# The compression's first layer in half-blocks with contiguous operands, in a hybrid decoder step on one core

## The chip, the cores and the metric

The kernel runs on one core of a Trainium2 chip. The metric is the device time in microseconds (us) of one execution. Each version is timed in several runs, and the median counts. The engines are TensorE (PE in the rows, its weight loads PEld), VectorE (DVE), ScalarE (ACT), GpSimd (POOL) and SyncE (SP, which issues the transfers). Each takes its instructions in the order written, and waits where one of them has to wait.

## The reference

One layer of a decoder for two groups of requests: a prompt of 1024 tokens and 8 samples of 8 new tokens, each sample with 512 tokens behind it in a paged cache. One projection feeds a gated convolution, a gated DeltaNet and a sparse attention with three branches (compressed, selected, window); then an output projection, a layer norm, a convolutional feed-forward block and another layer norm. All of it is in float32. The change concerns the compression of keys and values, for the prompt's tokens and for each sample's cached ones:

```python
def compress_blocks(rows, pe, w1, b1, w2):
    b, t_pad, kvh, hd = rows.shape
    r = rows.reshape(b, t_pad // CMP_STRIDE, CMP_STRIDE, kvh, hd)      # CMP_STRIDE = 16
    blocks = jnp.concatenate([r[:, :-1], r[:, 1:]], axis=2) + pe[:, None, :]
    hid = jax.nn.gelu(jnp.einsum('bclhd,lde->bche', blocks, w1) + b1)   # l = 0..31, d = e = 64
    return jnp.einsum('bche,ed->bchd', hid, w2)
```

A block is 32 tokens long and a new one starts every 16 tokens, so each token (but those at the ends) is in two blocks: in the first half of one and in the second half of the one before. There are 63 blocks for the prompt and 31 for each sample, for each of 2 heads, once for keys (v = 0) and once for values (v = 1). The part with `pe` is computed ahead, as a bias.

## The kernel before

The program is written as Python generators that are woven together, and then ordered by a planner: it simulates a timeline with its own costs, and fixes each engine's order before the program runs. So the pieces named below stand among the pieces of other phases in each engine's queue.

**Order of the work.** `phase_a` makes the projections, the DeltaNet's products and the rows of keys and values, which go to DRAM (`kw_d`). Near its end it allocates `kvl`, starts loading the rows of the compression (`c.rc`, tiles named `kc`) and of the other branches (`c.rk`, `kk`), and loads the compression's weights (`cmp_weights`: `cw1`, `cw2`). `attn_prep` then transposes and splits the rows for the prompt's attention beside the last steps of the DeltaNet's scan. After that three generators run by turns: `attn_units` (the prompt's attention in 32 units: masked scores `pas`, softmax, transposes `pat`, products with the values `pao`), `side` (the end of the scan; then `sample_compress`, `sample_select` and `phase_sample` for the 8 samples) and `filler` (`phase_part`, a part of the output projection, `pwq`). The output projection's rest and the feed-forward block follow.

**Banks of PSUM.** While these three run, the 8 banks are split: `mm` 2, `tp` 2, `aux` 2, `po` 1, `pt` 1. `sample_compress` and `phase_part` take turns at the one bank of `pt`; the DeltaNet's steps and the samples' selection and attention use the two of `aux`.

**The prompt's compression.** `cmp_tile` (L970) takes a tile of 128 tokens (`Rows.load`, L964, one transfer a tile), transposes the 64 columns of each of 4 (k/v, head) pairs, and copies the result twice into X: on ScalarE to partitions 0 to 63 (L976), on VectorE to partitions 64 to 127, one token on (L978, L980). So a column of X holds two neighbouring tokens. `compress_prompt` (L999) multiplies, for keys and for values, 16 weights (two tokens each) with columns of X that lie 16 apart, into `pch` (L1004). `gelu_hid` (L939) adds the bias on ScalarE (L945) and goes on with gelu; `pck` and `pcv` (L1013, L1019) are the second layer.

**The samples' compression.** `sample_compress` (L1299) does the same from the pages. For each of 8 samples 4 pages are loaded (`kvp`, L1313), 128 tokens by 128 columns (two heads), and transposed into `pcx` (L1314); ScalarE copies that to `sX` in the same order (L1315). The first layer (`psh`, L1325) takes both heads at once: its weight is block-diagonal, 64 by 64 for each head in a 128 by 128 tile, in one of two buffers `w1bd` that hold four positions each. They are filled with zeros once; the blocks are loaded (L1324, two transfers for every four positions) between the matmuls. 32 matmuls for keys and 32 for values add up in one bank of `pt`, each over 8 x 31 columns of `sX` that are 16 apart. Then come `gelu_hid` and the second layer (`psk`, `psv`). `sample_select` (`psg`, `psc`, `psi`) uses the compressed keys.

A float32 matmul stands in the trace as two records, each with a weight load; a transpose is one.

## Time and profile before

| | before |
|---|---|
| time, median of 3 runs | 1825.28 us (1819.19, 1825.28, 1825.39) |
| span of the profiled execution | 1818.8 us |
| TensorE busy | 1723.8 us (95%) |
| VectorE busy | 918.2 us (50%) |
| ScalarE busy | 653.7 us (36%) |
| GpSimd busy | 602.7 us (33%) |

The span is that of one execution taken by the hardware profiler, from its first to its last instruction. No time of that same execution is given beside it; the three runs shown lie 0.4 to 6.6 us above it. A busy share is an average over stages that have different limits, and matmuls are pipelined, so the sum of their durations says less than the distance between their starts.

### The profile page before, as it was taken

What the parts mean: (1) busy time and instruction counts of PE and PEld (TensorE: products, weight loads), DVE (VectorE), ACT (ScalarE), POOL (GpSimd) and SP (SyncE); (2) the same over time, 40 slices, a digit from 0 to 9 for tenths busy, and PEclk for the clock granted to TensorE, in tenths of its full rate; (3) what the DMA queues carried; (4) which work ended last, traced back from release to release, by engine and by line L of the source; (5) the groups of instructions that cost most, each with busy time, mean ns of one, the idle gap of its engine ahead of it and who ended that gap; (6) DMA issues with size and microseconds to landing.
All of it is one profiled execution on the core that took longest, in us unless ns stands there. A gap on an engine that the chain in (4) does not pass through costs nothing.

```text
span 1818.8 us, 26368 instructions
## 1 busy us (share of the span) xinstructions
PE 1723.8 (95%) x9807; PEld 1533.9 (84%) x9807; DVE 918.2 (50%) x2347; ACT 653.7 (36%) x1388; POOL 602.7 (33%) x489
## 2 busy tenths in 40 slices
PE   5999999988999999998889899999999999999995
PEld 5999989986876767877677889999999899999994
DVE  8334657365785747786666232333323323333338
ACT  4324542133584636465545312113112122131123
POOL 5312551222273313333255323224122232242226
PEclk9999999999699999999999999999999999999998
DMA  8412245545244414521346512112111121120102
GB/s 287 151 56 61 93 144 130 147 113 142 49 124 105 116 45 152 169 80 48 99 143 218 188 36 69 35 35 63 31 47 47 35 59 35 35 70 24 47 13 103
DMA packets 191846, 165.74 MB, mean 91 GB/s; under 512 B 56644, under 2 KB 163174, under 8 KB 191654
## 3 DMA queue, kind: packets, MB, share of 16 engines
q1 hardware_dynamic: 191718, 164.06, 30.2%
q8 instruction: 77, 1.26, 0.3%
q14 instruction: 51, 0.42, 0.1%
HBM read 121.17 MB, written 46.97 MB: 92 GB/s over the span
## 4 chain that ended last, share of the span: by engine, by line
PE 78%; DVE 8%; DMA 6%; issue 3%; ACT 2%; SPq 1%; POOL 1%; DVEq 0%; ACTq 0%; POOLq 0%
PE pd L202 5%; PE pd L203 5%; PE pd L201 5%; PE puv L202 5%; PE puv L203 5%; PE puv L201 5%; PE pug L203 4%; PE pug L202 4%; PE pug L201 4%; PE psh L1325 3%; DMA ax_d<-xo 2%; PE pas L1102 2%; PE pat L1161 2%; PE pao L1176 1%; PE pn L203 1%
## 5 line engine op out<-in xcount | busy, mean ns | idle before, releaser
L193 POOL TENSOR_TENSOR wlf<-wrf,whf 128x1024 fp32r<-128x1024 f32 x44 | 105.5, 2398 | 449.0 <-ACT whf L192 422.8
L1736 DVE TENSOR_TENSOR acc<-acc,pd 128x512 f32<-128x512 f32 x162 | 109.7, 686 | 224.5 <-PE pd L203 224.5
L1698 ACT COPY fg<-pug 128x384 f32<-128x384 f32 (+1 forms) x88 | 31.7, 388 | 431.2 <-PE pug L203 431.2
L201 PE MATMUL puv<-x1h,whf 128*128 128x384 f32 (+1 forms) x528 | 172.9, 328 | 5.0 <-ACT fg L1698 5.0
L202 PE MATMUL puv<-x1h,wlf 128*128 128x384 f32 (+1 forms) x528 | 173.0, 328 | 0.1
L201 PE MATMUL pug<-x1h,whf 128*128 128x384 f32 (+1 forms) x528 | 172.7, 327 | 0.2 <-ACT x1h L173 0.2
L203 PE MATMUL puv<-x1l,whf 128*128 128x384 f32 (+1 forms) x528 | 172.9, 327 | 0.0
L202 PE MATMUL pug<-x1h,wlf 128*128 128x384 f32 (+1 forms) x528 | 172.5, 327 | 0.0
L203 PE MATMUL pug<-x1l,whf 128*128 128x384 f32 (+1 forms) x528 | 172.3, 326 | 0.0
L202 PE MATMUL pd<-dh,hl 128*128 128x512 f32 (+1 forms) x396 | 155.6, 393 | 0.0
L203 PE MATMUL pd<-dl,hh 128*128 128x512 f32 (+1 forms) x396 | 155.3, 392 | 0.0
L201 PE MATMUL pd<-dh,hh 128*128 128x512 f32 (+1 forms) x396 | 152.0, 392 | 0.8 <-DVE acc L1734 0.8
L1137 POOL TENSOR_TENSOR ass<-ass,az 128x256 f32<-128x256 f32 (+6 forms) x56 | 70.8, 1284 | 186.9 <-DVE az L1131 133.5
L1102 PE MATMUL pas<-K,aq 128*128 128x320 f32 (+5 forms) x384 | 102.8, 371 | 4.8 <-DVE amx L1109 4.7
L201 PEld LDWEIGHTS puv<-x1h,whf 128*128 128x128 f32 x528 | 99.7, 189 | 6.3 <-ACT fg L1698 5.3
L1172 DVE TENSOR_TENSOR atl<-pat,ath 128x512 fp32r<-128x512 f32 (+1 forms) x136 | 89.9, 668 | 28.7 <-ACT ath L1170 27.7
L1170 ACT CAST ath<-pat 128x512 fp32r<-128x512 f32 (+1 forms) x136 | 75.7, 571 | 74.1 <-PE pat L1161 71.3
L202 PEld LDWEIGHTS pug<-x1h,wlf 128*128 128x128 f32 x528 | 99.1, 188 | 3.5
L203 PEld LDWEIGHTS pug<-x1l,whf 128*128 128x128 f32 x528 | 99.1, 188 | 2.9
L201 PEld LDWEIGHTS pug<-x1h,whf 128*128 128x128 f32 x528 | 99.1, 188 | 2.9 <-ACT x1h L173 0.3
L221 DVE SCALAR_TENSOR_TENSOR fz<-fg,w_f,fz 128x1024 f32<-128x1024 f32 x88 | 88.2, 1061 | 24.4 <-ACT fz L219 24.4
L202 PEld LDWEIGHTS puv<-x1h,wlf 128*128 128x128 f32 x528 | 99.6, 189 | 0.9 <-POOL wlf L193 0.5
(552 smaller groups left out, 4336.7 us busy)
## 6 DMA issues: line engine op xcount, KB each, us to landing
wrf<-in_w_up_dram SPq DMA_DIRECT2D x44, 512.0 KB
wdr<-in_w_down_dram SPq DMA_DIRECT2D x22, 512.0 KB
aq<-q_d SPq DMA_DIRECT2D x32, 256.0 KB
wra<-in_w_in_dram SPq DMA_DIRECT2D x14, 512.0 KB
xt<-in_x_prompt_dram SPq DMA_DIRECT2D x8, 512.0 KB
x_d<-xt SPq DMA_DIRECT2D x8, 512.0 KB
sv_d<-gsv SPq DMA_DIRECT2D x8, 512.0 KB
ma_d<-gma SPq DMA_DIRECT2D x8, 512.0 KB
```

The source lines that it names most:

```text
L193: c.nc.gpsimd.tensor_tensor(lo, raw, hi, op=OP.subtract)
L201: c.nc.tensor.matmul(out, ah(k), bh(k), start=start and j == 0, stop=False)
L202: c.nc.tensor.matmul(out, al(k), bh(k), start=False, stop=False)
L203: c.nc.tensor.matmul(out, ah(k), bl(k), start=False, stop=stop and j == n - 1)
L221: nc.vector.scalar_tensor_tensor(o, src(i), wcol(i), o, op0=OP.mult, op1=OP.add)
L1102: nc.tensor.matmul(p[:, :step], u.q[:, h, 4 * kv + g0 + g], c.K[:, kk, ks], start=h == 0, stop=h == 1)
L1137: nc.gpsimd.tensor_tensor(x[:, g, :n], x[:, g, :n], z[:, b, g:g + 1].to_broadcast([128, n]), op=OP.mult)
L1161: nc.tensor.transpose(pt[:, a, g], (SW if b else SS)[:, g, t * 128:t * 128 + 128], c.ident)
L1170: nc.scalar.copy(th[:, :k], pt[:, :k])
L1172: nc.vector.tensor_tensor(tl[:, :k], pt[:, :k], th[:, :k], op=OP.subtract)
L1325: nc.tensor.matmul(p, w1[:, l % 4], X[:, :, l:l + 16 * 30 + 1:16], start=l == 0, stop=l == 31)
L1736: nc.vector.tensor_tensor(a, a, p[:r], op=OP.add)
```

## The change

A block is cut into its two halves of 16 tokens. Every group of 16 tokens is multiplied once with a weight that holds both halves side by side (64 columns for the first half, 64 for the second), and a block's hidden layer is the first half's product of its own group plus the second half's product of the next group. The tokens are stored so that each matmul reads its columns in one piece. For the samples each head is a matmul of its own over 64 rows, and the second head's accumulator lies in another bank. Docstrings go; the lines that only delete one are left out here, as is the constant `SX`, which has no use any more.

```diff
-KC = 3
+KC = 2
@@ phase_a
-            c.rc = Rows(c, c.kw_d[0:SP, 0:256], "kc")
+            c.rc = Rows(c, c.kw_d[0:SP, 0:256].rearrange("(q s) (j d) -> q j s d", s=2, d=64), "kc")
@@ cmp_weights
-    c.w1 = pool.tile([128, 2, 16, 64], F32, name="cw1")
+    c.w1 = pool.tile([128, 2, 8, 128], F32, name="cw1")
     for v in range(2):
-        nc.sync.dma_start(c.w1[:, v], I["cmp_w1"][0, v].rearrange("(m s) d e -> (s d) m e", s=2))
+        for f in range(2):
+            nc.sync.dma_start(c.w1[:, v, :, 64 * f:64 * f + 64],
+                              I["cmp_w1"][0, v, 16 * f:16 * f + 16].rearrange("(m s) d e -> (s d) m e", s=2))
@@ gelu_hid
-def gelu_hid(c, pool, parts, out, n):
-    x = pool.tile(n, F32, name="glx", bufs=1)
-    u = pool.tile(n, F32, name="glu", bufs=1)
-    for i, (p, bias) in enumerate(parts):
-        nc.scalar.activation(x[:, i] if len(parts) > 1 else x, p, AF.Identity, bias=bias)
+def gelu_hid(c, x, u, out):
@@ Rows.load
-            x = pool.tile([128, self.src.shape[1]], F32, name=self.name, bufs=n)
-            self.c.nc.sync.dma_start(x, self.src[self.t * 128:self.t * 128 + 128])
+            x = pool.tile([128] + list(self.src.shape[1:]), F32, name=self.name, bufs=n)
+            rows = slice(self.t * 128, self.t * 128 + 128)
+            if len(x.shape) == 2:
+                self.c.nc.sync.dma_start(x, self.src[rows])
+            else:
+                for a in range(2):
+                    self.c.nc.sync.dma_start(x[:, :, a], self.src[rows, :, a])
@@ cmp_tile
-    kd = c.rc.tiles[t].rearrange("p (j d) -> p j d", d=64)
-    p = c.ps.tile([64, 4, 128], F32, name="pkc", tag="mm", bufs=c.nb["mm"])
+    kd = c.rc.tiles[t]
+    p = c.ps.tile([128, 4, 128], F32, name="pkc", tag="mm", bufs=c.nb["mm"])
     for j in range(4):
-        nc.tensor.transpose(p[:, j], kd[:, j], c.ident)
-    nc.scalar.copy(X[0:64, :, t * 128:t * 128 + 128], p)
-    if t:
-        nc.vector.tensor_copy(X[64:128, :, t * 128 - 1:t * 128 + 127], p)
-    else:
-        nc.vector.tensor_copy(X[64:128, :, 0:127], p[:, :, 1:128])
+        nc.tensor.transpose(p[:, j], kd[:, j].rearrange("p s d -> p (s d)"), c.ident)
+    for j in range(2):
+        (nc.vector.tensor_copy if j else nc.scalar.copy)(
+            X[:, :, 2 * j:2 * j + 2, 16 * t:16 * t + 16].rearrange("p m j a -> p j a m"),
+            p[:, 2 * j:2 * j + 2].rearrange("p j (a m) -> p j a m", m=8))
@@ compress_prompt
-    p = c.ps.tile([64, 2, 2, 63], F32, name="pch", tag="aux", bufs=c.nb["aux"])
+    p = c.ps.tile([128, 2, 2, 64], F32, name="pch", tag="aux", bufs=c.nb["aux"])
     for v in range(2):
-        for m in range(16):
-            nc.tensor.matmul(p[:, v], c.w1[:, v, m], X[:, 2 * v:2 * v + 2, 2 * m:2 * m + 16 * 62 + 1:16], start=m == 0, stop=m == 15)
+        for m in range(8):
+            nc.tensor.matmul(p[:, v], c.w1[:, v, m], X[:, m, 2 * v:2 * v + 2], start=m == 0, stop=m == 7)
+    x = pool.tile([64, 2, 2, 63], F32, name="glx")
+    u = pool.tile([64, 2, 2, 63], F32, name="glu")
+    for v in range(2):
+        nc.scalar.copy(u[:, v], p[64:128, v, :, 1:64])
+    for v in range(2):
+        nc.vector.scalar_tensor_tensor(x[:, v], p[0:64, v, :, 0:63], c.cbias[:, v:v + 1], u[:, v], op0=OP.add, op1=OP.add)
...
-    gelu_hid(c, pool, [(p[:, v], c.cbias[:, v:v + 1]) for v in range(2)], hids[:, :, :, 0, 0:63], [64, 2, 2, 63])
+    gelu_hid(c, x, u, hids[:, :, :, 0, 0:63])
@@ attn_prep
-        X = cp.tile([128, 4, SP], F32, name="X")
-        c.rc.load(cp, 8 - KC)
+        X = cp.tile([128, 8, 4, 64], F32, name="X")
+        c.rc.load(cp, 4 - KC)
         c.rk.load(cp, 8 - KK)
-        for t in range(8):
+        for t in range(4):
             cmp_tile(c, t, X)
@@ sample_compress
-    w1bd = [tmp.tile([128, 4, 128], F32, name=f"w1bd{i}") for i in range(2)]
-    for x in w1bd:
-        nc.gpsimd.memset(x, 0.0)
     for v in range(2):
-        X = tmp.tile([128, NB, 512], F32, name="sX", bufs=SX)
+        w1 = tmp.tile([128, 16, 2, 64], F32, name="sw1")
+        X = tmp.tile([128, 16, NB, 32], F32, name="sX")
...
-            nc.scalar.copy(X[:, b], p.rearrange("p g t -> p (g t)"))
+            nc.scalar.copy(X[:, :, b], p.rearrange("p g (a l) -> p l (g a)", l=16))
+            if b == 1:
+                for h in range(2):
+                    for f in range(2):
+                        nc.sync.dma_start(w1[64 * h:64 * h + 64, :, f], I["cmp_w1"][0, v, 16 * f:16 * f + 16].rearrange("l d e -> d l e"))
             if b % 2:
                 yield SY
-        p = c.ps.tile([128, NB, 31], F32, name="psh", tag=PT, bufs=c.nb[PT])
-        for l in range(32):
-            w1 = w1bd[l // 4 % 2]
-            if l % 4 == 0:
-                for h in range(2):
-                    x = slice(64 * h, 64 * h + 64)
-                    nc.sync.dma_start(w1[x, :, x], I["cmp_w1"][0, v, l:l + 4].rearrange("l d e -> d l e"))
-            nc.tensor.matmul(p, w1[:, l % 4], X[:, :, l:l + 16 * 30 + 1:16], start=l == 0, stop=l == 31)
-            if l == 15:
-                yield SY
+        ph = [c.ps.tile([128, NB, 32], F32, name=f"psh{h}", tag=(PT, "aux")[h], bufs=c.nb[(PT, "aux")[h]]) for h in range(2)]
+        for l in range(16):
+            for h in range(2):
+                r = slice(64 * h, 64 * h + 64)
+                nc.tensor.matmul(ph[h], w1[r, l].rearrange("p f e -> p (f e)"), X[r, l], start=l == 0, stop=l == 15)
+        yield SY
+        x = tmp.tile([128, NB, 31], F32, name="glx")
+        u = tmp.tile([128, NB, 31], F32, name="glu")
         hid = tmp.tile([128, NB, 31], F32, name="shid")
-        gelu_hid(c, tmp, [(p, c.sbias[:, v:v + 1])], hid, [128, NB, 31])
+        nc.scalar.copy(u[0:64], ph[0][64:128, :, 1:32])
+        nc.scalar.copy(u[64:128], ph[1][0:64, :, 0:31])
+        nc.vector.scalar_tensor_tensor(x[0:64], ph[0][0:64, :, 0:31], c.sbias[0:64, v:v + 1], u[0:64], op0=OP.add, op1=OP.add)
+        nc.vector.scalar_tensor_tensor(x[64:128], ph[1][64:128, :, 1:32], c.sbias[64:128, v:v + 1], u[64:128], op0=OP.add, op1=OP.add)
+        gelu_hid(c, x, u, hid)
```

## Rows read from the trace of the kernel before

**Rows 1.** The page: the span, and busy time, share and instructions of each engine.

```profile
span 1818.8 us, 26368 instructions
...
PE 1723.8 (95%) x9807; PEld 1533.9 (84%) x9807; DVE 918.2 (50%) x2347; ACT 653.7 (36%) x1388; POOL 602.7 (33%) x489
```

**Rows 2.** Stretches: from:to, length, busy us of each engine, granted clock, DMA, GB/s.

```profile
432.00:447.00 15.00, 14.56 (x71) 10.29 (x70) 1.55 (x6) 1.03 (x4) 2.54 (x4) 1.00 0.12 40
...
450.00:505.00 55.00, 53.53 (x277) 46.31 (x277) 39.34 (x164) 28.99 (x128) 16.36 (x26) 0.66 0.30 63
...
560.00:600.00 40.00, 40.00 (x155) 25.51 (x153) 17.57 (x58) 16.12 (x52) 10.90 (x12) 0.97 0.22 57
600.00:640.00 40.00, 36.99 (x268) 33.05 (x266) 32.53 (x98) 25.79 (x66) 16.46 (x14) 1.00 0.40 117
640.00:680.00 40.00, 40.00 (x165) 25.95 (x164) 15.90 (x64) 10.92 (x25) 5.64 (x6) 1.00 0.15 38
```

**Rows 3.** The chain of waits, pieces in order of time: start, us, what.

```profile
432.76 13.81 PE pch L1004 x64
...
608.44 0.59 PE psc L1393 x16
...
648.90 3.36 PE psh L1325 x8
```

**Rows 4.** TensorE's timeline: start, us, line, op, tiles, records (x).

```profile
428.59 1.06 PE L732 MATMUL pg<-gt,gY 128*128 128x128 f32 x8
...
563.58 6.87 PE L1325 MATMUL psh<-sX,w1bd 128*128 128x248 f32 x16
```

**Rows 5.** Tile pkc, its instructions: duration min/median/max in ns, first and last start.

```profile
L975 PE MATMUL pkc<-ident,kc x32: 272/273/299, 381.8 to 416.1; 128*64 128x128 f32 x32
L976 ACT COPY X<-pkc x8: 578/578/581, 383.0 to 416.4; 64x512 f32<-64x512 f32 x8
L978 DVE COPY X<-pkc x7: 674/684/685, 387.9 to 417.9; 64x512 f32<-64x512 f32 x7
```

**Rows 6.** TensorE's timeline, DeltaNet's state products of 64 rows: one head, then two.

```profile
483.94 2.07 PE L816 MATMUL pgs<-gs,gwq 64*128 64x512 f32 x2
...
488.81 2.08 PE L816 MATMUL pgs<-gs,gwq 64*128 64x512 f32 x4
```

**Rows 7.** TensorE's timeline around the samples' scores, weights of 64 columns.

```profile
720.34 0.56 PE L1102 MATMUL pas<-K,aq 128*128 128x320 f32 x2
720.83 1.10 PE L1452 MATMUL pss<-skw,qs 128*64 128x256 f32 x8
721.86 0.56 PE L1102 MATMUL pas<-K,aq 128*128 128x320 f32 x2
722.26 0.39 PE L201 MATMUL pwq<-wqh,yqh 128*128 128x512 f32 x1
```

**Rows 8.** Timeline of all engines around the end of pch; idle time before in brackets.

```profile
431.57 0.48 DVE L800 SCALAR_TENSOR_TENSOR gy<-pgy,gcol,gate 128x256 f32<-128x256 f32 x1
...
446.65 0.61 ACT L945 ACTIVATE glx<-pch,ccb 64x126 f32<-64x126 f32 x2 [12.85 <-PE pch L1004]
447.30 0.41 DVE L946 TENSOR_TENSOR glu<-glx 64x252 f32<-64x252 f32 x1 [12.84 <-ACT glx L945]
...
449.51 0.40 PE L1013 MATMUL pck<-chid,cw 64*64 64x128 f32 x2 [2.96 <-DVE chid L951]
```

**Rows 9.** ScalarE's groups by form, 300 to 900: busy us, mean ns, idle before.

```profile
L1180 ACT COPY aot<-pao 64x256 f32<-64x256 f32 x28 | 10.3, 366 | 26.7 <-PE pao L1176 26.1
L1315 ACT COPY sX<-pcx 128x512 f32<-128x512 f32 x16 | 9.4, 584 | 3.2 <-PE pcx L1314 3.1
```

**Rows 10.** VectorE's groups by form: reductions of contiguous and of strided elements.

```profile
L592 DVE TENSOR_REDUCE grn<-gsq 128x8 f32<-128x512 f32 x8 | 5.5, 681 | 5.6 <-ACT gsq L590 5.5
...
L1060 DVE TENSOR_REDUCE aca<-acs 128x128 f32<-128x512 f32 x4 | 4.3, 1076 | 0.0
```

**Rows 11.** SyncE's queue, 350 to 700: waited for, us in total, times, longest.

```profile
SPq L1324 <- PE psh L1325: 25.2, 8, 5.1
```

**Rows 12.** A stretch in which the weights of the prompt's compression loaded (columns as in rows 2).

```profile
298.00:301.00 3.00, 3.00 (x19) 3.00 (x18) 2.82 (x8) 0.00 (x0) 0.00 (x0) 1.00 1.03 234
```

More of the change, by code (lines that the diff above doesn't have):

```diff
@@ L42 @@
 XB = 1
-SX = 1
 S1 = 400
```

## Prediction

> **What bounds the kernel now.** I read the page's busy shares first, then the stretches, then the chain of waits, then TensorE's own timeline around the two places that the change touches. TensorE is busy for 95% of the span [rows 1]; no other engine comes near. So TensorE time that goes away can come off the end, unless another engine's chain takes over in that stage, and the stages have to be looked at one by one.
>
> The prompt's first layer (pch) lies in 432 to 447 us: TensorE is full, VectorE and ScalarE have next to nothing to do, because everything behind pch is queued after it [rows 2]. The chain of waits goes straight through it, 13.81 us [rows 3]. The samples' first layer (psh) lies in two stages, 560 to 600 and 640 to 680: TensorE 40.00 of 40, VectorE only 17.57 and 15.90. In the stage between them, with no psh, TensorE has 36.99 and VectorE 32.53 of 40 [rows 2]. In the psh stages attention is starved by psh in TensorE's queue, and the chain again runs through psh [rows 3]. These are places where TensorE sets the end.
>
> **The matmuls, one by one.** A float32 matmul stands as two records. psh has 128 of them in 12 runs of 16 or 8; a run of 8 takes 3.36 us of the chain [rows 3], 0.42 us a record for 248 columns. pch has 64: 13.81 / 64 = 0.216 us for 126 columns [rows 3]. Both read their moving operand 16 elements apart. A float32 matmul that reads it contiguously costs half: eight records of 128 columns in 1.06 us, of which the last one's 0.27 us [rows 5] is drain, so (1.06 - 0.27) / 7 = 0.11 us [rows 4]. For 256 columns I take 0.22.
>
> Prompt: 2 x 8 matmuls, 32 records of 128 columns, 32 x 0.11 = 3.5 us for 13.8: 10.3 us less.
>
> Samples: the count stays at 128 records (16 positions x 2 heads x 2 for keys and values, two records each), of 256 contiguous columns, but each uses 64 rows, and neighbours sit on opposite row halves and in different PSUM banks. What does such a pair cost? The trace has this very shape once: gated-delta state products with 64 rows and 128 weight columns. One head alone, two records, took 2.07 us; two heads on opposite row halves, four records, took 2.08 us [rows 6]. So opposite halves run at the same time. With that, 64 pairs x 0.22 = 14.1 us. Bounds: 14.1 if every pair overlaps, 128 x 0.22 = 28.2 if none does. I take 14.1, because the row is of the same form, with psh's alternation between halves.
>
> The Trainium skill speaks against this: TensorEngine Tiling (Tiling Modes, Key Properties) says that a change of tiling mode drains TensorE, and psh's runs are interleaved with full-array attention matmuls; it gives no figure.
>
> What a change of shape costs can be read where the sample attention uses column halves: four pairs of 256 and 264 columns start at 720.83, and the next full matmul at 721.86, 1.03 us for 4 x 0.217 = 0.87; before them two 320-column records hold the engine for 0.49 us, after them two such take 0.40 (721.86 to 722.26) [rows 7]. So a visit costs 0.16 + 0.09 = 0.25 us; with 12 runs as now, 3 us. I charge it: 17 us for the samples, against 128 x 0.42 = 53.8 now. TensorE gets back 36.8 us (22.6 if no pair overlaps).
>
> **How much of it reaches the end.** Each psh stage has 64 records, 26.9 us, and so 13.1 us of other TensorE work. With 8.5 us of psh in its place, at the occupancy of the stage between them (36.99 / 40 = 0.925), it takes 21.6 / 0.925 = 23.4 us. VectorE's work, at its share there (32.53 / 40 = 0.81), needs 21.6 and 19.6 us [rows 2], so it is close behind but not the bound. Each stage loses 16.6 us: 33 us for both. Without overlap it is (13.1 + 15.6) / 0.925 = 31 us, so 18 for both.
>
> **The rest of the change.** Behind pch, ScalarE's two bias steps (0.61 us together) become two copies of the upper half, followed by two additions on VectorE. Then comes the rest of gelu, during which TensorE waits for its next product until 449.51 [rows 8]. The copies are the same size as the steps they replace; the additions, of 126 columns against 0.41 us for 252, are about 0.3 us each by that row, 0.6 us on the chain. Net for pch: 10.3 - 0.6 = 9.7 us. The same addition in the samples costs about 1.2 us each time (two copies of some 0.37 [rows 9] for one step, two additions for none); attention's matmuls queued around cover it, and it is 2.4 us if they don't.
>
> Transposes of the prompt's rows: 32 become 16 (16 x 0.11 = 1.8 us of TensorE); 8 copies of 0.58 us on ScalarE and 8 of 0.68 on VectorE [rows 5] become four and four of 128x256, 0.37 on ScalarE [rows 9] and 0.48 on VectorE by the nearest row [rows 8]. They write with a stride. No copy with such a stride is in the trace; the nearest row is a reduction that reads with one, 1.08 us against 0.68 for the same 128x512 [rows 10], a factor of 1.58. So VectorE gets back 5.5 - 1.9 = 3.6 us (2.4 at the factor), ScalarE 3.1 (2.3). Beside the gated-delta scan, which has waits of its own, I count 2 us (0 to 4).
>
> The 16 copies into sX (0.58 us each [rows 9]) now read PSUM 16 elements apart: nothing at one bound, and 16 x 0.58 x 0.58 = 5.4 us more ScalarE work at the factor of rows 10. The Trainium skill, SBUF (State Buffer), in the note on cachelines under Door 1, says that PSUM's lines are two float32 wide and that non-contiguous PSUM access slows matmuls; of ScalarE it says nothing, and no run here shows it. ScalarE has room in the stages where half of the copies run (25.79 of 40 [rows 2]).
>
> Loads: the samples' weights come as four transfers of 256 KB each time, issued ahead of most pages, where 16 of 64 KB were fed between the matmuls. The bytes stay: 1 MB each time. SyncE's queue waited 25.2 us for psh to free those buffers, and the query loads stood behind [rows 11]; that wait goes. The prompt's weights came in the same 256-byte pieces; while they loaded, the stretch 298 to 301 moved 234 GB/s [rows 12], so 1 MB takes 4.5 us, and pages behind it are late by up to that. The prompt's rows now come in 256-byte pieces too, 1 MB in all; half of it is loaded early, under projections that fill TensorE [rows 12]. For strided copies and loads together I charge 2 us (0 to 9). The second accumulator takes one of the two banks of the samples' score products; those (psc, 0.59 us of the chain [rows 3]) must wait until the values' half is freed. Nothing, as they are needed after that half anyway; 0.6 us if not. The zero fill of the old weights and two more small issues lie on idle engines: nothing.
>
> Sum: 2 + 9.7 + 33 - 2 = 43 us. The profiled span of 1818.8 us [rows 1] becomes 1776. The three runs shown are 0.4, 6.5 and 6.6 us above that span; with the median's 6.5 the forecast is **1782 us**, 2.4% less than 1825.28. A difference of 0.5% (9 us) is about what a measurement of this kernel can tell from none.
>
> **The rivals.**
> *No overlap* (17%): the scheduler puts other matmuls between the halves, or the halves' weight loads wait for each other. For it: each half now has its own weight loads. Against it: rows 6. The sum is 2 + 9.7 + 18 - 2 = 28: 1797 us.
> *The weight burst* (14%): the last pages land 4.5 us late twice, TensorE having nothing else then. For it: the burst stands in the same queue. Against it: attention's matmuls are there to fill in. 43 - 9 = 34: 1791 us.
> *All comes back, and clock too* (10%): psh's 36.8 us return whole, and the stretch 450 to 505 us, where the granted clock was 0.66 on the mean [rows 2] (it went between 1.2 and 2.4 GHz, after TensorE had waited for gelu), keeps the higher level. VectorE's 39.34 us there, at a share of 0.81, need 48.5 us, so at most 6.5 of the 55 come back: 43 + 3.8 + 6.5 = 53: 1772 us.
> *The clock the other way* (9%), the case on the other side: with the steady psh stream gone, TensorE sits at 1.2 GHz in more of the attention phase. Where TensorE is the bound, each us of its work then takes two, so a stretch of x us at the lower level loses x / 2. The change comes out even at 86 us more of it, and slower by over 0.5% from 104 us on. The stretch 450 to 505 alone, if it fell to 1.2 GHz throughout, takes 55 x 0.66 / 0.5 = 73 us, 18 more: 1800 us. I give that size 4%, no measurable change 3%, slower 2%. Against it: during psh itself the clock stood at 0.97 and 1.00, and so it did in the psh-less stage between [rows 2].
>
> My forecast keeps 50%.
>
> **Range and chances.** From everything returned with the clock at best and the best bounds (another 2 + 2 us, and the lowest of the three offsets: 1762) to no overlap with the bad bounds of copies and loads (28 - 7 = 21: 1804): 1762 to 1804 us. Faster by over 0.5%: 0.94, as every case but part of the last is; within 0.5%: 0.04; slower: 0.02.
>
> **What would show it.** psh records in pairs a few ns apart, a run of 16 in about 1.8 us in place of 6.87 [rows 4]; pch in 3.5 us; VectorE's share in the psh stages up from 0.4 to 0.8; no SyncE wait for psh. Wrong would be: pairs one after the other at 0.22 each, sX copies near 0.9 us, TensorE waiting for the weight load, or long stretches of 1.2 GHz where there were none.

## The result, and the profile after

The changed kernel takes 1792.97 us, the median of 4 runs (1785.16 to 1801.30), against 1822.39 us for the kernel before in 4 runs of the same comparison: a ratio of 0.9837, with a 95% interval of 0.9812 to 0.9861. It is 1.6% or 29 us faster. The forecast was 1782 us, a gain of 43: it is faster, as forecast, by two thirds of the amount. The profiled execution took 1793.5 us with a span of 1791.8.

The page of the changed kernel: span, TensorE's busy time, and the granted clock in 40 slices.

```profile
span 1791.8 us, 26213 instructions
...
PE 1696.1 (95%) x9759; PEld 1527.1 (85%) x9759; DVE 918.9 (51%) x2349; ACT 650.6 (36%) x1386; POOL 602.2 (34%) x487
...
PEclk8999999998679999998899999999999999999998
```

TensorE is still busy for 95% of the span, and VectorE's total has hardly moved [rows 1]: no other engine has become the bound. The slices of the clock, 44.8 us each, say more: counted from 0, slices 9 to 11 (403 to 538 us) stand at 0.8, 0.6 and 0.7, and 18 and 19 (806 to 896 us) at 0.8. In the page of the kernel before, slice 10 alone was low in the middle, at 0.6.

The stretches that answer to [rows 2], same columns.

```profile
432.00:447.00 15.00, 11.73 (x74) 10.94 (x73) 6.75 (x26) 3.10 (x10) 2.54 (x4) 0.79 0.79 157
450.00:505.00 55.00, 54.42 (x262) 44.54 (x261) 40.97 (x170) 30.64 (x126) 21.72 (x33) 0.65 0.24 54
560.00:600.00 40.00, 37.44 (x232) 31.26 (x232) 26.87 (x81) 20.91 (x60) 15.63 (x16) 0.91 0.59 133
600.00:640.00 40.00, 39.40 (x301) 34.55 (x300) 29.64 (x102) 23.12 (x62) 13.06 (x12) 1.00 0.28 86
640.00:680.00 40.00, 38.11 (x242) 32.02 (x244) 31.67 (x126) 25.61 (x62) 11.38 (x10) 1.00 0.58 170
```

Where psh used to hold TensorE, VectorE now works 26.87 and 31.67 us of 40 instead of 17.57 and 15.90: attention is no longer starved, as forecast. But in this profile 432 to 447, which ran at full clock before, stands at 0.79, and 560 to 600 fell from 0.97 to 0.91.

The timeline of the changed kernel around the two first layers; idle time before in brackets.

```profile
430.39 2.23 PE L1005 MATMUL pch<-X,cw 128*128 128x128 f32 x18
433.35 1.73 PE L1005 MATMUL pch<-X,cw 128*128 128x128 f32 x14
435.17 0.42 ACT L1009 COPY glu<-pch 64x126 f32<-64x126 f32 x2 [3.57 <-PE pch L1005]
435.62 0.60 DVE L1011 SCALAR_TENSOR_TENSOR glx<-pch,ccb,glu 64x126 f32<-64x126 f32 x2 [1.39 <-ACT glu L1009]
...
438.78 0.40 PE L1020 MATMUL pck<-chid,cw 64*64 64x128 f32 x2 [3.27 <-DVE chid L948]
...
570.84 7.18 PE L1331 MATMUL psh<-sX,sw 64*128 64x256 f32 x64
577.95 0.38 PE L1183 MATMUL pao<-atl,V 128*128 128x256 f32 x1
```

pch takes 3.96 us in two pieces (13.81 before [rows 3]), and pck starts at 438.78 instead of 449.51 [rows 8], 10.7 us earlier. psh for the keys is one unbroken run: 64 records in 7.18 us, 0.22 us a pair of records. Before, 16 records took 6.87 us [rows 4]. Both psh runs together hold TensorE for 14.36 us, against 55.55 before. The rows of psh alone, the kernel before first (stretch, then busy us of PE, PEld and the engines that read it):

```profile
380.00:1000.00 620.00, 55.55 (x128) 25.34 (x128) 0.92 (x2) 0.96 0.40 114
```

```profile
380.00:1000.00 620.00, 14.36 (x128) 12.22 (x128) 1.89 (x4) 1.44 (x4) 0.91 0.43 124
```

The copies that write or read with a stride in the changed kernel (min/median/max in ns, first and last start).

```profile
L979 ACT COPY X<-pkc x4: 599/614/682, 380.4 to 416.5; 128x256 f32<-128x256 f32 x4
L979 DVE COPY X<-pkc x4: 593/596/603, 384.8 to 417.3; 128x256 f32<-128x256 f32 x4
...
L1320 ACT COPY sX<-pcx x16: 562/588/606, 526.7 to 621.3; 128x512 f32<-128x512 f32 x16
```

The row copies move 256 elements a partition where they moved 512, and cost 0.61 and 0.60 us (ScalarE, VectorE) where [rows 5] had 0.58 and 0.68: on ScalarE nothing is saved. The strided write is what is new in them; no run tries it apart. The sX copies, which now read PSUM 16 elements apart, have a median of 588 ns; before, it was 586 (mean 584 [rows 9]): nothing.

The chain of waits still runs through both (start, us, what), so TensorE still sets the pace there.

```profile
430.56 2.06 PE pch L1005 x18
...
570.84 7.18 PE psh L1331 x64
```

**Three parts of the time.** The changed products gave back what the prediction said, and more; so where did 13 us go? For every profile here I split the time from its start to the last product of the feed-forward block (pd) into three parts, counted from the trace's records: TensorE's *work*, its busy time with what it did at 1.2 GHz counted half; the *lower clock*, the other half of that time; and *idle*. A row of the windows gives the same to its two digits: in the row of 439 to 585 us shown with the fifth experiment, (1 - 0.78) x 146 = 32 us go to the lower clock, 135 - 32 = 103 are work, and 146 - 135 = 11 idle.

| kernel | median us | ratio to before | work | lower clock | idle | sum |
|---|---|---|---|---|---|---|
| before | 1822.4 | | 1689.6 | 34.1 | 76.8 | 1800.5 |
| before, row copies swapped | 1827.4 | 1.0019 | 1687.9 | 41.7 | 77.4 | 1807.0 |
| changed | 1793.0 | 0.9837 | 1640.8 | 55.3 | 77.8 | 1773.9 |
| changed, again | 1793.1 | 0.9849 | 1646.0 | 40.8 | 81.4 | 1768.2 |
| changed, row copies swapped | 1790.8 | 0.9817 | 1642.5 | 46.7 | 82.0 | 1771.2 |
| changed, halves swapped | 1795.1 | 0.9840 | 1644.8 | 51.9 | 83.6 | 1780.2 |
| prompt's half | 1830.8 | 1.0039 | 1682.8 | 39.1 | 82.1 | 1804.1 |
| prompt's half, row copies swapped | 1823.2 | 0.9997 | 1677.6 | 44.6 | 81.4 | 1803.6 |
| samples' half | 1799.3 | 0.9861 | 1654.3 | 39.2 | 86.1 | 1779.6 |
| heads in turn | 1815.6 | 0.9958 | 1659.6 | 48.2 | 84.1 | 1791.9 |
| half the weight loads | 1797.9 | 0.9856 | 1644.6 | 55.0 | 84.1 | 1783.7 |
| scores twice | 1800.0 | 0.9872 | 1651.8 | 52.5 | 79.2 | 1783.5 |
| prompt's sum four times | 1809.5 | 0.9922 | 1654.9 | 49.2 | 85.3 | 1789.5 |
| psh in four steps | 1803.5 | 0.9905 | 1654.3 | 43.7 | 85.3 | 1783.2 |

The last three columns before the sum are one profiled execution each, and not always a middle one: that of the prompt's half took 1823.9 us, 7 below its kernel's median, and that of heads in turn 1811.6, 4 below. Nor are the parts independent. Between the two executions of the changed kernel, whose instructions and order on TensorE are the same, the lower clock falls by 14.5 us, but work rises by 5.2 and idle by 3.6, so that the sum falls by 5.7 only. So single rows are to be read with care, and means over several are good to a few us.

### The profile page after: what moved, and what is told of

Read it like the earlier page. It is cut to its first block, busy times and chain, and to the rows that moved or that the text cites. A ratio compares the mean times of both kernels' runs of the same rounds, so it can differ in the third digit from the quotient of the medians.

```text
span 1791.8 us, 26213 instructions
## 1 busy us (share of the span) xinstructions
PE 1696.1 (95%) x9759; PEld 1527.1 (85%) x9759; DVE 918.9 (51%) x2349; ACT 650.6 (36%) x1386; POOL 602.2 (34%) x487
## 4 chain that ended last, share of the span: by engine, by line
PE 78%; DVE 7%; DMA 6%; POOL 3%; ACT 3%; issue 2%; SPq 1%; DVEq 0%; POOLq 0%; ACTq 0%
PE pd L201 5%; PE pd L202 5%; PE pd L200 5%; PE puv L201 5%; PE puv L202 5%; PE puv L200 5%; PE pug L202 4%; PE pug L201 4%; PE pug L200 4%; PE pas L1109 2%; PE pat L1168 2%; DMA wrf<-in_w_up_dram 1%; PE pao L1183 1%; PE pn L202 1%; PE pn L200 1%
## 5 line engine op out<-in xcount | busy, mean ns | idle before, releaser
L1109 PE MATMUL pas<-K,aq 128*128 128x320 f32 (+5 forms) x384 | 106.2, 380 | 7.2 <-DVE amx L1116 6.6
L202 PEld LDWEIGHTS puv<-x1l,whf 128*128 128x128 f32 x528 | 99.5, 188 | 0.0
```

Source lines behind the costliest of these rows:

```text
L202: c.nc.tensor.matmul(out, ah(k), bl(k), start=False, stop=stop and j == n - 1)
L1109: nc.tensor.matmul(p[:, :step], u.q[:, h, 4 * kv + g0 + g], c.K[:, kk, ks], start=h == 0, stop=h == 1)
```

## The experiments

All have the changed kernel as their base unless said otherwise, and were timed against the kernel before on the same chip (1822.9 to 1823.4 us there).

**The changed kernel again, no edit.**

> The changed kernel again, nothing edited: the yardstick for the runs beside it. The profile of the changed kernel gives three theories for the 12 us by which it fell short of the forecast. Clock: from the end of the prompt's row transposes to the end of the output projection TensorE's work shrank by 48 us counted at 2.4 GHz, about as forecast, but 43 us more of it ran at 1.2 GHz, which gives 22 us back. Chain: attention's own VectorE and ScalarE steps set the pace once psh is gone. Burst: the 1 MB of weights ahead of the pages makes psh late. Expected: ratio to the kernel before 0.981 to 0.986; by the clock theory the time at the lower level is 45 us or more above that of the kernel before in each profile (mean granted clock 0.963 to 0.970 against 0.976), by the other two the two clocks may come out alike.

Measured: 1793.06 us, ratio 0.9849 (0.9810 to 0.9888), the same as the first time. The clock did not come out as the clock theory had it: the lower level cost 40.8 us in this profile, 14.5 less than in the first, and the span was 5.7 us shorter. So the first profile overstated it. What holds over many executions is this. In 57 executions of the kernel before (three sets) the mean granted clock was 0.972 to 0.973; in the 10 of the changed kernel 0.966; with the two order-only edits below (10 executions) 0.969. The share left out, times the spans, is 49 to 51 us lost to the lower level before, 61 in the changed kernel and 56 with the edits of order. And the time goes along with it: of 23 executions of the kernel before, the three at a clock of 0.966 had spans of 1829.4 to 1832.3 us, the four at 0.975 had 1815.0 to 1820.3 (the one at 0.978 had 1821.8). A straight line through all 57 rises by 0.69 us of span for each us lost, one through the ten of the changed kernel by 0.80. That is an association: whatever lets the clock fall may also make an execution longer by itself.

**The prompt's half alone.** The samples' first layer as in the kernel before.

```
-        for l in range(16):
-            for h in range(2):
-                r = slice(64 * h, 64 * h + 64)
-                nc.tensor.matmul(ph[h], w1[r, l].rearrange("p f e -> p (f e)"), X[r, l], start=l == 0, stop=l == 15)
...
+        for l in range(32):
...
+            nc.tensor.matmul(p, w1[:, l % 4], X[:, :, l:l + 16 * 30 + 1:16], start=l == 0, stop=l == 31)
```

> Only the prompt's half of the change; the samples' first layer is as in the kernel before. The sum gave 10 us for this half (2 + 9.7, less some of the strided loads). Clock theory: the profile of the changed kernel has 12 us more at 1.2 GHz between 416 and 510 us, worth 6, so 3 to 8 us faster than before. Chain theory and burst theory: both put the loss into the samples' stages, so the full 10 us faster, within 2.

Measured: 1830.83 us, ratio 1.0039 (1.0019 to 1.0059): slower by 7 us, which no theory had. pck starts at 440.7, 9 us earlier than before, but the stores of the attention's tiles stand at 497, 531, 586, 640 us against 504, 532, 583, 639: the lead is used up by the second tile. Part of the loss goes along with the clock: over the 12 executions it was 0.969 on the mean, against 0.972 for the kernel before beside them.

**The samples' half alone.** The prompt's compression as in the kernel before.

```
-        for m in range(8):
-            nc.tensor.matmul(p[:, v], c.w1[:, v, m], X[:, m, 2 * v:2 * v + 2], start=m == 0, stop=m == 7)
+        for m in range(16):
+            nc.tensor.matmul(p[:, v], c.w1[:, v, m], X[:, 2 * v:2 * v + 2, 2 * m:2 * m + 16 * 62 + 1:16], start=m == 0, stop=m == 15)
```

> Only the samples' half of the change; the prompt's compression is as in the kernel before. The sum gave 33 us for it. Clock theory: 20 to 26 us faster than before, with psh in pairs as in the changed kernel, and at least 20 us more of TensorE's time at 1.2 GHz than in the kernel before, before and after the psh runs. Chain theory: 18 to 24 us faster with the time at 1.2 GHz as in the kernel before. Burst theory: 24 us (33 - 9), with TensorE waiting for pages ahead of psh.

Measured: 1799.33 us, ratio 0.9861 (0.9827 to 0.9895), 24 us faster. All three theories had given about this time; the second marks of two of them failed: the lower clock costs 39.2 us in the profile, 5 more than in the kernel before where the clock theory wanted at least 10, and TensorE waited only 1.2 us for pages between 520 and 645 us. The chain theory's mark, a clock as before, is met within what profiles differ by (34.1 and 41.7 in the two of the kernel before). The table puts 9 us into idle time (86.1 against 76.8). The longest share of it that the waits of that stretch show is 4.8 us, nine times, for VectorE to pass over the scores: a piece of what the chain theory says.

**Heads in turn.**

```
-        for l in range(16):
-            for h in range(2):
+        for h in range(2):
+            for l in range(16):
```

> The changed kernel with the two loops of psh swapped: all 16 positions of one row half, then all of the other. Neighbours no longer sit on opposite halves, so each psh record stands alone: 128 x 0.216 = 28 us of TensorE where the pairs took 14. Clock theory: TensorE sets the end there, and the 14 us come on top, less a few if TensorE then keeps 2.4 GHz for longer: 8 to 15 us slower than the changed kernel. Chain theory: TensorE has room, at most 4 us slower. Burst theory: TensorE had nothing to do but psh while the pages were late, so the full 14.

Measured: 1815.56 us, ratio 0.9958, 22 us slower than the changed kernel: more than the longest that any theory gave. psh's run in the timeline of this kernel:

```profile
566.99 13.32 PE L1331 MATMUL psh<-sX,sw 64*128 64x256 f32 x64
```

64 records take 13.32 us instead of 7.18. That is the price of the pairing, read directly: 12.3 us over both runs (26.65 against 14.36 in all). It falls to TensorE in full, which the chain theory excludes; another 10 us come on top that the psh matmuls themselves don't explain.

**Half the weight loads.**

```
-                for h in range(2):
-                    for f in range(2):
-                        nc.sync.dma_start(w1[64 * h:64 * h + 64, :, f], I["cmp_w1"][0, v, 16 * f:16 * f + 16].rearrange("l d e -> d l e"))
+                for f in range(2):
+                    nc.sync.dma_start(w1[0:64, :, f], I["cmp_w1"][0, v, 16 * f:16 * f + 16].rearrange("l d e -> d l e"))
+                nc.gpsimd.tensor_copy(w1[64:128], w1[0:64])
```

> The changed kernel with half of the samples' weight loads: only the copy for one head comes from memory (two transfers, 512 KB each time), GpSimd copies it to the other head's 64 partitions. In the changed kernel's profile TensorE waited 4.3 us for pages. Burst theory: the pages land earlier and psh with them, 4 to 9 us faster than the changed kernel. Clock theory and absorption theory (the stages behind the change have a pace of their own, by VectorE's passes over the scores and by the order in which the planner put attention and samples, so that TensorE time freed ahead of them or beside them returns only in part): within 4 us.

Measured: 1797.88 us, ratio 0.9856 (0.9819 to 0.9892): not faster. The copy in this kernel, a row of its tile (min/median/max in ns, first and last start):

```profile
L1324 POOL COPY sw<-sw x2: 1885/1889/1893, 535.1 to 596.2; 64x2048 f32<-64x2048 f32 x2
```

And what pcx waited for there, in us and times, with the same line of the changed kernel's first profile behind it:

```profile
  DMA kvp<-in_cache_nsa_kv_dram: 3.9, 5
```

```profile
  DMA kvp<-in_cache_nsa_kv_dram: 4.3, 3
```

psh starts at 582.0 here, 11 us later than in the first profile of the changed kernel, and yet the whole is only 5 us slower, within both intervals. The pages are waited for longer than before the change (0.6 us there), but by about as much with half of the bytes as with all; and with all of the bytes the two kernels with another order, below, waited only 1.6 and 2.0 us. So fewer bytes brought neither an earlier psh nor a faster kernel, and nothing here speaks for this rival; with six executions on each side, a gain of a few us could still hide in the noise. That psh's own start does not set the end is what this one profile suggests; it is not shown.

**Scores twice.**

```
-            for h in range(2):
-                nc.tensor.matmul(p[:, :step], u.q[:, h, 4 * kv + g0 + g], c.K[:, kk, ks], start=h == 0, stop=h == 1)
+            for r in range(2 if i < 3 else 1):
+                for h in range(2):
+                    nc.tensor.matmul(p[:, :step], u.q[:, h, 4 * kv + g0 + g], c.K[:, kk, ks], start=h == 0, stop=h == 1)
```

> The changed kernel with the score products of the first three query tiles issued twice into the same bank: (1 + 2 + 3) x 4096 columns, 10 us more TensorE work at 2.4 GHz, in the stretch 441 to 585 us, where the changed kernel stood at 1.2 GHz for 64 us in one profile and 46 in another. Clock theory in its strong form (TensorE falls to 1.2 GHz there because it has too little to do, and the time follows the clock): the time at the lower level falls by 20 us or more and the kernel is no slower than the changed one, perhaps 5 us faster. If TensorE's work is what sets the pace there whatever the clock: 10 us slower. Absorption theory: 3 us slower or less, the clock as before.

Measured: 1800.02 us, ratio 0.9872 (0.9831 to 0.9914), 7 us slower, though the intervals overlap. The stretch from the start of attention to the end of the first psh, in the changed kernel, in its second profile and here, then the stretch from the end of the samples to the end of the output projection in the second profile and here (busy us of PE, PEld, DVE, ACT, POOL, then the clock):

```profile
439.00:585.00 146.00, 135.27 (x734) 112.11 (x733) 99.80 (x359) 82.55 (x287) 59.08 (x76) 0.78 0.44 98
```

```profile
438.00:583.00 145.00, 129.83 (x736) 106.99 (x736) 100.29 (x360) 83.27 (x288) 59.21 (x76) 0.84 0.44 99
...
837.00:958.00 121.00, 105.48 (x577) 86.21 (x577) 81.18 (x195) 66.12 (x119) 57.44 (x33) 0.97 0.50 158
```

```profile
442.00:590.00 148.00, 136.96 (x848) 117.17 (x848) 103.16 (x366) 84.76 (x293) 58.65 (x76) 0.88 0.44 99
849.00:974.00 125.00, 112.08 (x580) 91.01 (x580) 80.29 (x197) 66.94 (x120) 58.01 (x33) 0.92 0.48 155
```

With more to do, TensorE kept the higher clock for a little more of the first stretch in this profile (0.88), and lost as much later, where nothing was edited (0.92 against 0.97). Neither says much: the four profiles of the changed kernel, other orders included, stand at 0.78 to 0.86 from 439 to 585 us and at 0.90 to 0.97 from 837 to 958. Over six executions the mean clock was 0.967, as without the edit (0.966). The strong form of the clock theory falls: the time at the lower level is not removed by giving TensorE more work in the place where it was seen.

**The prompt's sum four times.**

```
     for v in range(2):
-        for m in range(8):
-            nc.tensor.matmul(p[:, v], c.w1[:, v, m], X[:, m, 2 * v:2 * v + 2], start=m == 0, stop=m == 7)
+        for r in range(4):
+            for m in range(8):
+                nc.tensor.matmul(p[:, v], c.w1[:, v, m], X[:, m, 2 * v:2 * v + 2], start=m == 0, stop=m == 7)
```

> The changed kernel with the prompt's first layer multiplied four times into the same bank, one after the other: 128 records in place of 32, 13.8 us as in the kernel before, so 10 us more of TensorE in that place, all else as changed. If pch's time returns one for one, as the forecast had it: 10 us slower than the changed kernel. Absorption theory (the prompt's half alone brought nothing: 7 us slower than before): at most 3 us slower, the later start used up by the third query tile.

Measured: 1809.48 us, ratio 0.9922 (0.9903 to 0.9941), 16 us slower for 10.9 us more in pch. The timeline:

```profile
431.61 2.23 PE L1006 MATMUL pch<-X,cw 128*128 128x128 f32 x18
434.57 3.29 PE L1006 MATMUL pch<-X,cw 128*128 128x128 f32 x28
438.13 9.32 PE L1006 MATMUL pch<-X,cw 128*128 128x128 f32 x82
...
450.91 0.65 PE L1021 MATMUL pck<-chid,cw 64*64 64x128 f32 x2 [3.46 <-DVE chid L948]
```

So absorption falls as well: here pch's time reaches the end in full and more. But TensorE has the same work at that place as in the samples' half alone (13.87 us of pch there), and the two kernels are 10 us apart. In the table their work and idle time agree within 1 us, and the 10 us stand under the lower clock (49.2 and 39.2). Over six executions each the mean clock was 0.967 and 0.970, which is 5 us of lost time; so the clock goes along with about half of it, and the rest is open.

**psh in four steps.**

```
                 nc.tensor.matmul(ph[h], w1[r, l].rearrange("p f e -> p (f e)"), X[r, l], start=l == 0, stop=l == 15)
-        yield SY
+            if l % 4 == 3:
+                yield SY
```

> The changed kernel with psh's sixteen positions handed over in four steps of four, so that the planner may put attention's matmuls between them. If attention starves while the runs of 7 us hold TensorE, as it did in the kernel before: 3 to 6 us faster. If the pairs' visits cost 0.25 us each as the prediction charged: 8 visits instead of 2, 1.5 us of TensorE. Clock theory: within 4 us.

Measured: 1803.52 us, ratio 0.9905 (0.9881 to 0.9928), 10 us slower; the interval just touches that of the changed kernel's second set (0.9810 to 0.9888). The planner put nothing between the steps, and did something else instead, as the two psh runs show:

```profile
569.12 7.18 PE L1331 MATMUL psh<-sX,sw 64*128 64x256 f32 x64
...
629.17 11.60 PE L1331 MATMUL psh<-sX,sw 64*128 64x256 f32 x64
```

In the second run one half's records stand alone for the first 4.4 us, one every 0.216 us, until the other half's begin (at 633.60). The planner had parted the halves. The prediction's rival "no overlap" exists: whether the pairs stand side by side is the planner's choice in each build, not the program's.

**Four kernels with another order and the same work.** Three swap the engines of the row copies (in the kernel before, in the prompt's half and in the changed kernel; the line is that of the last two); one issues the halves of each psh position the other way round.

```
-        (nc.vector.tensor_copy if j else nc.scalar.copy)(
+        (nc.scalar.copy if j else nc.vector.tensor_copy)(
```

```
-            for h in range(2):
+            for h in (1, 0):
```

> The kernel before with one edit that changes no work: the two copies of each transposed row tile trade engines (ScalarE 0.58 us, VectorE 0.68 us each, both kinds of equal number). The runs so far don't add up: the prompt's half alone made the kernel 7 us slower, yet giving the prompt's first layer its old 13.8 us again inside the changed kernel cost 16, and the samples' half with the old first layer is 10 us faster than that. Order theory: the planner answers any edit with another order of the attention's, the scan's and the samples' pieces, and the order alone is worth some 5 to 10 us either way; of TensorE's order 144 lines differ here from the kernel before, fewer than in the other three of this set, so within 5 us here. Rival (each half has a price of its own, the clock and the chain set it): within 3 us of the kernel before.

> The run with the prompt's half alone, with the same kind of edit: of the two copies of each row tile (0.61 us on ScalarE, 0.60 on VectorE) each goes to the other engine. 1355 lines of TensorE's order differ from that run's. Order theory: 4 us or more away from that run's 1831 us, and if towards the forecast for this half (10 us faster than before), its slower time came from the order. Rival: 1831 within 3 us, the prompt's half is slower by itself.

> The changed kernel with the same swap of the two row copies. 735 lines of TensorE's order differ. Order theory: 4 us or more away from the changed kernel's 1793 us, either way. Rival: within 3 us of it.

> The changed kernel with the two row halves of each psh position issued in the opposite order, the pairs as before. 1070 lines of TensorE's order differ. Order theory: 4 us or more away from the changed kernel's 1793 us, either way. Rival: within 3 us of it.

Measured: 1827.41 us for the kernel before with the swap (ratio 1.0019, 0.9998 to 1.0040), 4 us up; 1823.19 for the prompt's half (0.9997, 0.9979 to 1.0015), 7.6 us down (on another chip, each against the kernel before there), its interval clear of the 1.0019 to 1.0059 that the same half had without the swap; 1790.81 and 1795.11 for the changed kernel (0.9817 and 0.9840), within 3 us. So the order theory holds for one of the four clear of the noise; the first, 4 us up, is not clear of it; and for the two of the changed kernel its mark of 4 us failed and the rival's "within 3 us" held. In the prompt's half the traded copies take as long on the other engine (medians of 597 ns on ScalarE and 589 on VectorE), so the order is what is left to explain the 7.6 us. A new order with the same work can be worth that much, enough for the 7 by which the prompt's half seemed to harm. Whether order also makes the rest of the 10 us between the samples' half and the sum four times is not shown.

## Why the prediction was right, and where it missed

**The time that TensorE gets back: right.** psh fell by 41.2 us (55.55 to 14.36), where 36.8 was forecast, and pch by 9.9, where 10.3 was. The overlap of row halves, read from two heads of the DeltaNet [rows 6], carried over to psh as it stood; had it not, the heads-in-turn run says that the kernel would have been 22 us slower (the prediction had 15), 12.3 of them in psh itself. The Trainium skill, TensorEngine Tiling (Array Packing), Tiling Modes, Key Properties, says that tiles work independently and that a change of mode drains TensorE; the runs show the first (64 records in 7.18 us side by side, in 13.32 one half after the other), and what they leave for the second is 0.2 us a run, as follows.

**The visits: mis-sized.** I charged 12 visits of 0.25 us. There are two, of 0.2 us: the next product starts 7.11 us after psh's first record, and 32 pairs at 0.216 us are 6.91. That the planner left the runs whole because no weight loads had to be fed between the matmuls any more is my reading; cut into four steps, they stayed whole too.

**The strided copies: both bounds were asked for, and each hit once.** Reading PSUM with a stride cost nothing (a median of 588 ns, before 586); writing with one cost ScalarE 0.61 us where 0.37 was the row for a contiguous copy of that size. By these rows the eight row copies together cost 1.4 us more than at the contiguous prices (0.37 and 0.48).

**Loads: right to charge little.** No wait of SyncE for psh is left, and halving the weight loads brought nothing (1797.9 against 1793.1 us).

**How much of it reaches the end: this is where it missed, by the clock and by attention's own products.** In the table the kernel before stands twice, the changed kernel four times. The means are 1688.8, 37.9 and 77.1 us for work, lower clock and idle, against 1643.5, 48.7 and 81.2. So work fell by 45.2, idle rose by 4.1, and the lower clock took 10.8: together 30.3 us, the measured gain. The forecast's own terms, on the same lines, were 10.3 + 1.8 + 36.8 = 48.9 less work, and 6 lost to idle time and other steps (an occupancy of 0.925, gelu, strided copies): 43.

The first two parts, 45.2 - 4.1 = 41.1, agree with it to 2 us, but that is partly luck. Counted by tile on the same means, each record by the time that it adds after the one before it has ended, psh gave back 39.3, pch 10.2 and pkc 2.0: 51.5 us, 2.6 more than forecast. Attention's products with scores and values (pas, pao), as many as before, took 7.4 more. Their own durations did not grow (pas: 102.9 and 107.6 us of busy time before, 103.1 to 106.2 after; pao: 130.8 and 130.6 before, 128.5 to 137.2 after, with more of both at 1.2 GHz); they overlap less with the records before them. The sum had them unchanged. Why they overlap less is not tested; part of it may be that psh's ends used to cover their starts. The row of pas alone (PE, PEld, DVE), in the kernel before and in the changed kernel's second profile:

```profile
380.00:1000.00 620.00, 102.85 (x384) 65.10 (x384) 98.58 (x224) 0.96 0.40 114
```

```profile
380.00:1000.00 620.00, 103.62 (x384) 64.11 (x384) 98.32 (x224) 0.94 0.44 126
```

The 10.8 us of lower clock is the other term that the forecast had not. By the mean clocks of all executions it is 6 to 11 us lost, and at 0.7 to 0.8 us of span for each, some 4 to 9 of the 13 missing; this is an estimate from the two lines fitted above. The prediction named that mechanism as a rival, "the clock the other way", with 9%, and saw it as a case of its own, 18 us in the stretch of 450 to 505. The profiles show it elsewhere. The granted clock in three stretches, the two profiles of the kernel before first (the second with the row copies swapped), then the four of the changed kernel in the order of the table:

| us | before | changed | prompt's half, two | samples' half |
|---|---|---|---|---|
| 403 to 448 | 1.00, 0.99 | 0.84, 0.86, 0.86, 0.84 | 0.80, 0.84 | 0.93 |
| 450 to 505 | 0.66, 0.66 | 0.65, 0.84, 0.79, 0.78 | 0.78, 0.75 | 0.72 |
| 806 to 896 | 0.96, 0.97 | 0.88, 0.92, 0.91, 0.89 | 0.98, 0.96 | 0.92 |

The stretch that the prediction looked at kept its clock in the first profile and rose in the other three, by 6 us on the mean of the four. The loss lies around pch (403 to 448, 6.5 us), where it comes mostly with the prompt's half, and late in the attention phase (806 to 896, 6 us), where it comes with the samples' half; in the first, TensorE was busy for 39.2 and 39.5 us of 45 before and for 37.5 to 38.8 after. Around pch, as the rows have it, before and in the changed kernel's first profile (PE, PEld, DVE, ACT, POOL, then the clock):

```profile
403.00:448.00 45.00, 39.49 (x251) 30.69 (x250) 25.93 (x66) 16.87 (x41) 11.76 (x16) 1.00 0.41 122
```

```profile
403.00:448.00 45.00, 38.40 (x243) 33.42 (x243) 27.81 (x80) 17.09 (x47) 10.05 (x14) 0.84 0.64 156
```

By 806 to 896 us the changed kernel is at other work than the kernel before was at that time.

The Trainium skill, TensorE: Matmul & The Clock Gate, Terms, prices time at the lower clock at the share of pulses left out, half of it at 1.2 GHz; the runs show 0.69 and 0.80 of that in the span, and between the two profiles of the changed kernel 5.7 of 14.5 us. What brings the clock down more often after the change is open: more work in the place where it was seen did not change it over the whole.

**The prompt's 9.7 us: right on its stretch, not by itself at the end.** Alone it brings nothing (the two kernels of the prompt's half: 0.9997 and 1.0039). By the table (for the half without the swap, the row of one of its fastest executions) their work fell by 8.6 us, the lower clock took 3.9 back and idle time 4.7. On top of the samples' half it brings 6 (1799.3 to 1793.1, the intervals overlap), and taken away inside the changed kernel it costs 16. The forecast lies between, and no single run measures its true price, since each comes with another order.

**The rivals.** No overlap: not in the changed kernel, but in half of psh's time when its steps were cut in four. The weight burst: not borne out; half of the bytes brought no gain that these runs can tell. All back, and the clock too: its stretch did rise in three profiles of four, but the clock fell in others by more.

## What to carry to other kernels

Two matmuls on opposite row halves cost one if they stand side by side in the final order: look at the run's length in the timeline after every build (7.18, 11.60 and 13.32 us for the same 64 records). When a planner fixes the order, a part of a change tried alone also tries another order; time an edit that changes no work before reading anything under 8 us out of such a run. And split TensorE's busy time by its granted clock before you count on it: here 45 us of work went away and only 30 of time.

## What the runs showed of the hardware that was not expected

The share of time at 1.2 GHz varies between executions of one and the same kernel, and their spread goes along with it: a mean clock of 0.959 to 0.971 with spans of 1805.5 to 1786.1 us in six executions of the changed kernel. GpSimd copied 64 x 2048 float32 from one half of the partitions to the other in 1.89 us.
